# Row sums of 64 MiB: the last fifteen columns scaled on GpSimd, and every load tile on a 1024-byte boundary of SBUF

## The chip, the cores and the metric

The kernel runs on one core of one Trainium2 chip. The metric is device time in microseconds (us) of one execution; the profile's span is some 1.6 us shorter, as it runs from the first to the last instruction. Executions of one kernel on one chip scatter over 0.15 to 0.3 us, now and then more, and the whole change moves a quarter of a microsecond. So the times are read together with the profile, in which the duration of one instruction repeats to some 10 ns, and the stretch from the row's sum to the final sum to some 30 (1.40 to 1.43 us in the seven profiles below whose ends are alike).

## The reference

```python
def setup_inputs():
    batch, seq, dim = 32, 512, 1024
    return {"x": np.random.randn(batch, seq, dim).astype(np.float32), "divisor": float(dim)}

def reference(x, divisor):
    return (np.sum(x, axis=-1) / divisor).astype(np.float32)
```

16,384 rows of 1,024 fp32 are summed and scaled: 128 rows per partition, 67.1 MB in, 64 KB out.

## The kernel before

The first 112 rows of each partition stream through three big rotating buffers in loads of 14 rows. The last 16 come in ever smaller loads (8, 4, 2, 1 rows, then one row in three pieces pa, pb, pc), so that little work is left after the last byte. VectorE (DVE) sums most, ScalarE (ACT) some rows of the end.

```python
main = [(2, 0)] + [(14, 0)] * 6 + [(14, 4), (12, 5)]     # rows of a load, of which on ScalarE
last = [(8, 4), (4, 2), (2, 1)]
bulk = ctx.enter_context(tc.tile_pool(name="bulk", bufs=3))    # t: [P, 14, D], 57,344 B a partition
one = ctx.enter_context(tc.tile_pool(name="one", bufs=1))
res = one.tile([P, M], F32, name="res")
fin = one.tile([P, L], F32, name="fin")
q = one.tile([P, L], F32, name="q")
r = one.tile([P, L], F32, name="r")
nc.gpsimd.memset(r, 0.0)
# ... (t4, t2, row, pa, pb, pc are allocated behind these, at their loads)
c = 768
load(row, x_last[:, j, :])
act_sum(r[:, j : j + 1], row[:, c:], by=scale)                  # ScalarE
nc.vector.reduce_sum(out=q[:, j : j + 1], in_=row[:, :c], axis=AX)
a, b = 448, 704
load(pa, x_last[:, L - 1, :a]); load(pb, x_last[:, L - 1, a:b])  # (cut to two lines)
load(pc[:, : D - b], x_last[:, L - 1, b:])
# ... (res is scaled on GpSimd and stored)
act_sum(pc[:, D - b : D - b + 1], pa)
nc.vector.reduce_sum(out=pc[:, D - b + 1 :], in_=pb, axis=AX)
nc.vector.scalar_tensor_tensor(out=fin[:, : L - 1], in0=q[:, : L - 1], scalar=scale,
                               in1=r[:, : L - 1], op0=MULT, op1=ADD)
nc.vector.tensor_scalar(out=scaled, in0=pc, scalar1=scale, scalar2=0.0, op0=MULT, op1=ADD,
                        accum_out=fin[:, L - 1 :])               # the "final sum"
tc.keep_in_program_order(nc.sync.dma_start(out=o_last, in_=fin))
```

In the built program the three big buffers start 128 bytes past a 256-byte boundary of SBUF. The tiles t4, t2, row, pa, pb and pc, behind 640 bytes of small tiles, happen to start on one.

## Time and profile before

| | before |
|---|---|
| time, three runs | 161.41 us (161.30 to 161.44) |
| span of the profile | 159.8 us |
| row (last but one) landed | 156.16 us |
| pb, pc landed (landing records) | 157.02, 157.50 us |
| final sum started | 157.79 us |

The prediction below shows the lines that carry this. One more pair of DVE's timeline (columns: start, duration, instruction, idle time before it and its releaser):

```profile
106.47 15.09 DVE L153 TENSOR_REDUCE res<-t 128x14 f32<-128x14336 f32 x1 [1.85 <-DMA t<-in_x_dram]
123.41 10.82 DVE L153 TENSOR_REDUCE res<-t 128x10 f32<-128x10240 f32 x1 [1.85 <-DMA t<-in_x_dram]
```

From the first 14-row tile at 21.76 (shown in the prediction) to 123.41 there are six tiles in 101.65 us, 16.942 us each.

### The profile page before, as it was taken

To read this page: it belongs to the slowest core of one execution; us is meant where nothing else is said; L and a number is where in the kernel's file an instruction comes from. 1 tells how busy PE (TensorE), PEld (TensorE's weight loads), DVE (VectorE), ACT (ScalarE), POOL (GpSimd) and SP (SyncE) were. 2 spreads that over 40 slices of the span, in tenths; PEclk is the share of its full clock that TensorE was granted. 3 is DMA by queue.
4 is the path that set the end of the run, shared out by engine and by line. 5 is a ranking of instruction groups with operands and counts; after the bars stand their busy time and mean duration, and the time that the engine had idled before them with its cause. 6 is when DMAs were issued, how large, how long until landed. Compare 5 with 4: busy or idle time off the path is not lost.

```text
span 159.8 us, 139 instructions
## 1 busy us (share of the span) xinstructions
DVE 121.1 (76%) x17; ACT 19.6 (12%) x37; POOL 0.8 (0%) x6
## 2 busy tenths in 40 slices
DVE  0500059995999599978999599959995996494985
ACT  3000000000000000000000000000001900480973
POOL 0000000000000000000000000000000000001000
DMA  7999999978999999978999999978999999899993
GB/s 250 472 459 459 459 459 459 459 330 359 459 459 459 459 459 459 459 316 373 459 459 459 459 459 459 416 345 388 459 459 427 394 480 505 353 435 390 408 400 132
DMA packets 2592, 67.18 MB, mean 420 GB/s; under 512 B 544, under 2 KB 928, under 8 KB 1056
## 3 DMA queue, kind: packets, MB, share of 16 engines
q1 hardware_dynamic: 2592, 67.18, 98.0%
HBM read 67.11 MB, written 0.07 MB: 420 GB/s over the span
## 4 chain that ended last, share of the span: by engine, by line
DMA 76%; DVE 22%; SPq 1%; issue 0%; DVEq 0%
DMA t<-in_x_dram 56%; DMA row<-in_x_dram 21%; DVE res L153 20%; SPq L142 1%; DVE q L176 1%; DVE scaled L198 0%; DVE pc L193 0%; DVE fin L194 0%; DVEq L198 0%; DVEq L232 0%
## 5 line engine op out<-in xcount | busy, mean ns | idle before, releaser
L153 DVE TENSOR_REDUCE res<-t 128x14 f32<-128x14336 f32 (+3 forms) x9 | 111.2, 12360 | 34.3 <-DMA t<-in_x_dram 34.3
L147 ACT ACTIVATE junk<-t 128x1024 f32<-128x1024 f32 x16 | 16.2, 1013 | 135.9 <-DMA t<-in_x_dram 135.9
L153 DVE TENSOR_REDUCE q<-t 128x4 f32<-128x4096 f32 (+2 forms) x3 | 7.9, 2642 | 2.7 <-DMA t<-in_x_dram 2.5
L147 ACT ACTIVATION_READ_ACCUMULATOR junk<-t 128x1 f32 x16 | 3.0, 187 | 0.0
L147 ACT ACT_TABLE_LOAD x1 | 1.3, 1283 | 1.7 <-PEq L218 1.7
L189 POOL TENSOR_SCALAR res<-res 128x112 f32<-128x112 f32 x1 | 0.5, 494 | 143.8 <-DVE res L153 143.8
L176 DVE TENSOR_REDUCE q<-row 128x1 f32<-128x768 f32 x1 | 1.0, 953 | 0.0
L198 DVE TENSOR_SCALAR_CACHE_REDUCE scaled<-pc 128x322 f32<-128x322 f32 x1 | 0.5, 490 | 0.1
L147 ACT ACTIVATE junk<-pa 128x448 f32<-128x448 f32 x1 | 0.5, 548 | 0.0
L193 DVE TENSOR_REDUCE pc<-pb 128x1 f32<-128x256 f32 x1 | 0.4, 414 | 0.0
L147 ACT ACTIVATE junk<-row 128x256 f32<-128x256 f32 x1 | 0.4, 388 | 0.1
L194 DVE SCALAR_TENSOR_TENSOR fin<-q,r 128x15 f32<-128x15 f32 x1 | 0.2, 176 | 0.0
L147 ACT ACTIVATION_READ_ACCUMULATOR junk<-pa 128x1 f32 x1 | 0.2, 186 | 0.0
L147 ACT ACTIVATION_READ_ACCUMULATOR junk<-row 128x1 f32 x1 | 0.2, 185 | 0.0
L139 POOL MEMSET r<- 128x16 f32 x1 | 0.1, 112 | 1.3 <-POOLq L218 1.3
L218 POOL MEMSET const-bfloat16-1.0<- 128x1 bf16 x1 | 0.1, 103 | 0.0
L218 POOL MEMSET const-uint8-127<- 128x1 uint8 x1 | 0.1, 102 | 0.0
L218 POOL MEMSET const-float32-0.0<- 128x1 f32 x1 | 0.1, 99 | 0.2 <-issue 0.2
L218 POOL MEMSET const-float32-1.0<- 128x1 f32 x1 | 0.1, 99 | 0.0
L198 DVE DVE_READ_ACCUMULATOR scaled<-pc 128x1 f32 x1 | 0.1, 83 | 0.0
## 6 DMA issues: line engine op xcount, KB each, us to landing
t<-in_x_dram SPq DMA_DIRECT2D x7, 7168.0 KB, 35.7
t<-in_x_dram SPq DMA_DIRECT2D x1, 6144.0 KB, 33.3
t<-in_x_dram SPq DMA_DIRECT2D x1, 4096.0 KB, 26.1
t<-in_x_dram SPq DMA_DIRECT2D x2, 1024.0 KB, 18.6
t<-in_x_dram SPq DMA_DIRECT2D x1, 2048.0 KB, 30.5
row<-in_x_dram SPq DMA_DIRECT2D x1, 512.0 KB, 33.2
pa<-in_x_dram SPq DMA_DIRECT2D x1, 224.0 KB, 33.3
pc<-in_x_dram SPq DMA_DIRECT2D x1, 160.0 KB, 33.1
```

The lines of the kernel that those rows point to most:

```text
L139: nc.gpsimd.memset(r, 0.0)
L142: tc.keep_in_program_order(nc.sync.dma_start(out=dst, in_=src))
L147: nc.scalar.activation(junk[:, :n], src, COPY, scale=by, accum_out=dst)
L153: nc.vector.reduce_sum(out=dst[:, :d], in_=t[:, :d, :], axis=AX)
L176: nc.vector.reduce_sum(out=q[:, j : j + 1], in_=row[:, :c], axis=AX)
L189: nc.gpsimd.tensor_scalar_mul(out=res, in0=res, scalar1=scale)
L193: nc.vector.reduce_sum(out=pc[:, D - b + 1 :], in_=pb, axis=AX)
L194: nc.vector.scalar_tensor_tensor(out=fin[:, : L - 1], in0=q[:, : L - 1], scalar=scale, in1=r[:, : L - 1], op0=MULT, op1=ADD)
L198: nc.vector.tensor_scalar(out=scaled, in0=pc, scalar1=scale, scalar2=0.0, op0=MULT, op1=ADD, accum_out=fin[:, L - 1 :])
L218: nc = _bacc.Bacc("TRN2", target_bir_lowering=False, num_devices=1)
```

## The change

The intent is twofold. DVE's scaling of fifteen columns stands between the row's sum and the pb sum, at the end where the chain of waits is DVE alone; it goes to GpSimd, and 64 more columns of the row go to ScalarE. And a pad of 896 bytes, with the small tiles moved behind the load tiles, puts each tile that a load writes on a 1024-byte boundary.

```diff
+    pad = ctx.enter_context(tc.tile_pool(name="pad", bufs=1))
+    pad.tile([P, 224], F32, name="pad")
     bulk = ctx.enter_context(tc.tile_pool(name="bulk", bufs=3))
 ...
+    t4 = one.tile([P, 4, D], F32, name="t4")
+    t2 = one.tile([P, 2, D], F32, name="t2")
+    row = one.tile([P, D], F32, name="row")
+    a, b = 448, 704
+    pa = one.tile([P, 512], F32, name="pa")[:, :a]
+    pb = one.tile([P, b - a], F32, name="pb")
+    pc = one.tile([P, D - b + 16], F32, name="pc")[:, : D - b + 2]
     res = one.tile([P, M], F32, name="res")
 ...
-    r = one.tile([P, L], F32, name="r")
-    nc.gpsimd.memset(r, 0.0)
+    r = one.tile([P, 16], F32, name="r")[:, :1]
 ...
-    c = 768
+    c = 704
     load(row, x_last[:, j, :])
-    act_sum(r[:, j : j + 1], row[:, c:], by=scale)
+    act_sum(r, row[:, c:], by=scale)
 ...
-    nc.vector.scalar_tensor_tensor(
-        out=fin[:, : L - 1], in0=q[:, : L - 1], scalar=scale, in1=r[:, : L - 1], op0=MULT, op1=ADD
+    nc.gpsimd.tensor_scalar_mul(out=fin[:, :j], in0=q[:, :j], scalar1=scale)
+    nc.gpsimd.tensor_scalar(
+        out=fin[:, j : j + 1], in0=q[:, j : j + 1], scalar1=scale, scalar2=r, op0=MULT, op1=ADD
     )
```

More of the change, by code (lines that the diff above doesn't have):

```diff
@@ L165 @@
         else:
-            t = one.tile([P, rows, D], F32, name=f"t{rows}")
+            t = t4 if rows == 4 else t2
         load(t, x_last[:, j : j + rows, :])
@@ L169 @@
         j += rows
-    c = 768
-    row = one.tile([P, D], F32, name="row")
+    c = 704
     load(row, x_last[:, j, :])
-    act_sum(r[:, j : j + 1], row[:, c:], by=scale)
+    act_sum(r, row[:, c:], by=scale)
     nc.vector.reduce_sum(out=q[:, j : j + 1], in_=row[:, :c], axis=AX)
-    a, b = 448, 704
-    pa = one.tile([P, a], F32, name="pa")
-    pb = one.tile([P, b - a], F32, name="pb")
-    pc = one.tile([P, D - b + 2], F32, name="pc")
     load(pa, x_last[:, L - 1, :a])
```

## The prediction

> **What bounds the kernel now.** I first read the page's DMA rows and queue row, because a sum over 64 MiB ought to be bound by its loads.
>
> ```profile
> DVE 121.1 (76%) x17; ACT 19.6 (12%) x37; POOL 0.8 (0%) x6
> ...
> DMA  7999999978999999978999999978999999899993
> ...
> q1 hardware_dynamic: 2592, 67.18, 98.0%
> HBM read 67.11 MB, written 0.07 MB: 420 GB/s over the span
> ```
>
> The reader should see that the queue is busy for 98% of 16 engines' span, while VectorE (DVE) is busy for 76% and GpSimd (POOL) for nothing. The sevens in the DMA row look like holes in the stream, so the next view was DVE's timeline, to see whether they are real.
>
> ```profile
> 21.76 15.09 DVE L153 TENSOR_REDUCE res<-t 128x14 f32<-128x14336 f32 x1 [14.65 <-DMA t<-in_x_dram]
> 38.71 15.09 DVE L153 TENSOR_REDUCE res<-t 128x14 f32<-128x14336 f32 x1 [1.87 <-DMA t<-in_x_dram]
> 55.65 15.09 DVE L153 TENSOR_REDUCE res<-t 128x14 f32<-128x14336 f32 x1 [1.84 <-DMA t<-in_x_dram]
> 72.59 15.09 DVE L153 TENSOR_REDUCE res<-t 128x14 f32<-128x14336 f32 x1 [1.86 <-DMA t<-in_x_dram]
> ```
>
> Columns are start, duration, instruction, idle time before it and its releaser. Each reduce starts when its tile lands, 16.94 or 16.95 us after the one before, and the one that spans the first seven (32 to 40 us) comes after the same 16.94 us. The sevens are therefore an effect of binning whole row packets of 2.1 us. A tile is 128 x 57,344 B = 7.34 MB, so the stream runs at 7.34 MB / 16.94 us = 433 GB/s without a gap. DVE idles 1.85 us a tile: nothing that shortens its work in the main loop can help.
>
> So only two things set the end: when the last loads land, and what follows them. The end is in the chain of waits and the timeline.
>
> ```profile
> 122.91 33.25 DMA row<-in_x_dram
> 156.16 0.02 issue
> 156.18 0.96 DVE q L176
> 157.14 0.03 issue
> 157.17 0.18 DVE fin L194
> 157.34 0.34 DVE pc L193
> 157.68 0.04 DVEq L198
> 157.72 0.07 issue
> 157.79 0.49 DVE scaled L198
> ```
>
> ```profile
> 156.18 0.39 ACT L147 ACTIVATE junk<-row 128x256 f32<-128x256 f32 x1
> ...
> 156.72 0.55 ACT L147 ACTIVATE junk<-pa 128x448 f32<-128x448 f32 x1
> 157.17 0.18 DVE L194 SCALAR_TENSOR_TENSOR fin<-q,r 128x15 f32<-128x15 f32 x1
> 157.20 0.19 ACT L147 ACTIVATION_READ_ACCUMULATOR junk<-pa 128x1 f32 x1
> 157.26 0.41 DVE L193 TENSOR_REDUCE pc<-pb 128x1 f32<-128x256 f32 x1
> 157.79 0.49 DVE L198 TENSOR_SCALAR_CACHE_REDUCE scaled<-pc 128x322 f32<-128x322 f32 x1
> ...
> 158.31 0.34 SPq L201 DMA_DIRECT2D out_dram<-fin  x1
> ```
>
> ```profile
> pc<-in_x_dram SPq DMA_DIRECT2D x1, 160.0 KB, 33.1
> pb<-in_x_dram SPq DMA_DIRECT2D x1, 128.0 KB, 33.1
> ```
>
> The penultimate row lands at 156.16. From there the chain is DVE alone: sum of 768 columns, fifteen-column scaling, sum of pb, final scaled sum. The last piece, pc, was issued at 124.39 and landed 33.1 later, at 157.49 (pb: 123.87 + 33.1 = 156.97). The final sum thus starts about 0.30 us after its data is there: this slack is what the change can win from DVE. ScalarE's share is in at 157.20 + 0.19 = 157.39, GpSimd has been idle since 146.
>
> [...] In the built program the three big buffers start at byte 16,512, which is 128 past a boundary, but the tiles t4, t2 and row stand at multiples of 256 (768 past a multiple of 1024). The packet records give a median of 309 ns for the first load's 8,192-byte rows (off boundary) and 309 ns for each of t2's 128 (on one). [...]
>
> **The change part by part.**
>
> *Scaling moves to GpSimd.* DVE loses one instruction. By starts it costs 157.26 - 157.17 = 0.09 us, plus 0.03 of issue before it; without it the pb sum no longer waits for the row's sum to be visible, only for pb at 156.97. GpSimd gains two: fourteen columns, which can run from about 156.2, and one column with a per-partition addend, which needs the row's sum. GpSimd's only comparable instruction, 128x112, took 494 ns. I take 0.3 to 0.5 us for each, an estimate from that row.
>
> *Split of the row, 768 to 704 on DVE.* DVE's slope from its own rows: (1220 - 953) ns / (1024 - 768) = 1.04 ns a column, so 64 columns are 0.067 us. ScalarE's slope: (548 - 388) / (448 - 256) = 0.83 ns, so it gains 0.053 us; its row part with the readout then ends near 156.74, its pa sum near 157.44.
>
> *The new end, landings unchanged.* Row sum 156.18 + 0.886 = 157.07; pb sum starts then or up to 0.05 earlier, as DVE overlapped the start of the last pair by 0.09; it ends about 157.45 to 157.48; the same 0.12 us of semaphore and issue as now, so the final sum starts near 157.58 instead of 157.79. pc at 157.49 and ScalarE at 157.44 are both in. Gain about 0.21 us, capped near 0.27 by pc. GpSimd's last instruction would run from about 157.15 to 157.65, well before the final sum is read out at 158.28 - 0.21 = 158.07: hidden.
>
> *Alignment.* All loads stay in the same order and sizes. The packets fit bytes at 27.2 GB/s per engine plus about 8 ns: 8,192 B is 301 + 8 = 309, and 57,344 B is 2,108 + 8 = 2,116, the most frequent record. Each engine moves 16 loads x 8 rows = 128 such packets, so the whole overhead is 128 x 8 ns = 1.05 us. If half of it[...] came from misalignment, 0.60 us would go; if it is fixed, nothing. The equal 309s argue for nothing, with one reservation: no load tile of before stands on 1024, so a rule that needs 1024 is untested. I count 0.1 us on average.
>
> *Removed memset of r, and the pad.* The memset ran on idle GpSimd at the start, and the pad is never touched: zero. The order of instructions shows the same three loads hoisted ahead of the body and the same queue order after them.
>
> Sum: 161.41 - 0.21 - 0.10 = 161.1 us.
>
> **The rivals.** First, *alignment pays in full*: every landing moves up to 0.6 us forward, the tail follows as a block, the end is near 161.41 - 0.21 - 0.60 = 160.6. For it: the stream sets the end, so any saving in it counts in full. Against it: the equal packet times[...]. Second, *GpSimd becomes the last*: its two instructions, or a slow read of the addend r, end after DVE's final sum. It would need more than 158.07 - 157.15 = 0.9 us for one column, nearly twice its 112-column instruction; each tenth beyond is a tenth lost, so 161.3 to 161.6. Third, *pc's landing or ScalarE takes the place of DVE*: the gain is cut to what the new wait allows. pc caps it at 0.27 and so does not bite; ScalarE would, only if its pa sum slipped past 157.5 (now 157.39, expected 157.44). That would give 161.25 to 161.35. Fourth, the removed work changes nothing because the store waits elsewhere: the earlier result store, queued behind all loads, must also land before the last store; in the event records it does at 157.73, before 158.07, so it does not bite either.
>
> **Range and chances.** The tail alone with no alignment gain, 161.2, gets some 60%; some alignment gain, down to 160.6, about 25%; a new wait or chip-to-chip scatter above 161.35 about 15%. The three runs of before spread over 0.14 us. I say 161.1 us, with 160.5 to 161.4 for eight in ten. Two per cent is 3.2 us, and neither the stream[...] nor a tail of 3.6 us offers that: 2% for faster, 1% for slower, 97% for within 2%.
>
> **What would show it.** In the profile of the changed kernel, the 14-row reduces should still start 16.94 us apart. If alignment pays in full, they should start 8 x 4.7 ns = 0.04 us closer, at 16.90, and the row should land near 155.6. The row's reduce should last 0.886 us, the pb sum follow it without a gap, and the final sum start 0.2 us sooner after the row's landing: 1.42 us instead of 1.63. GpSimd should show two short instructions ending before the final sum. I would be wrong if the last store is released by GpSimd, if ScalarE or pc ends DVE's last wait before a start later than 157.7, or if the spacing of the big tiles changes by more than 0.1 us.

The sum: 161.41 - 0.21 - 0.10 = 161.1 us. Its 0.21 is worked out from the trace of before; its 0.10 is the weighing between nothing and 0.60. The 0.60 is an estimate, and not quite the half it is called: 128 bytes more in a packet, the buffers' displacement, would take 4.7 ns at the 27.2 GB/s that the packets fit, and an engine has 128 packets; that a displaced start costs as much was a supposition. That the stream at 433 GB/s had little left to give, and that GpSimd would not hold DVE up, were assumptions: the trace of before shows neither.

## The result, and the profile after

161.11 us median of six runs (161.04 to 161.20), against 161.32 (161.24 to 161.44) for the kernel before in six runs: ratio 0.9986, 95% interval 0.9973 to 0.9999. Run again beside the displaced kernels below, it gave 161.02 (160.97 to 161.25) against 161.38: ratio 0.9979 (0.9967 to 0.9991). A ratio is the mean time of one kernel's fast runs over that of the other's of the same rounds, so not quite the ratio of the quoted medians. The gain is 0.2 to 0.35 us, within 2%.

The page of the changed kernel: GpSimd has one instruction more on balance, the stream is as full as before.

```profile
DVE 120.9 (76%) x16; ACT 19.6 (12%) x37; POOL 1.2 (1%) x7
...
q1 hardware_dynamic: 2592, 67.18, 98.1%
```

DVE's timeline of the changed kernel, first and seventh 14-row tile:

```profile
21.77 15.09 DVE L163 TENSOR_REDUCE res<-t 128x14 f32<-128x14336 f32 x1 [14.60 <-DMA t<-in_x_dram]
...
123.31 10.82 DVE L163 TENSOR_REDUCE res<-t 128x10 f32<-128x10240 f32 x1 [1.88 <-DMA t<-in_x_dram]
```

101.54 us for the same six tiles, 16.923 each: 0.02 us closer, 0.11 us over the six. The end of the timeline:

```profile
156.12 0.89 DVE L185 TENSOR_REDUCE q<-row 128x1 f32<-128x704 f32 x1
156.17 0.26 POOL L199 TENSOR_SCALAR fin<-q 128x14 f32<-128x14 f32 x1 [10.10 <-DVE q L163]
...
156.98 0.42 DVE L198 TENSOR_REDUCE pc<-pb 128x1 f32<-128x256 f32 x1
157.10 0.27 POOL L200 TENSOR_SCALAR fin<-q,r 128x1 f32<-128x1 f32 x1 [0.67 <-DVE q L185]
157.12 0.19 ACT L157 ACTIVATION_READ_ACCUMULATOR junk<-pa 128x1 f32 x1
157.52 0.49 DVE L204 TENSOR_SCALAR_CACHE_REDUCE scaled<-pc 128x322 f32<-128x322 f32 x1
157.93 0.08 DVE L204 DVE_READ_ACCUMULATOR scaled<-pc 128x1 f32 x1
158.04 0.34 SPq L207 DMA_DIRECT2D out_dram<-fin  x1
```

The row's sum takes 0.886 us instead of 0.953 and the pb sum overlaps its end. From the start of the row's sum to that of the final sum (the tail, below) it is now 157.52 - 156.12 = 1.40 us; before it was 157.79 - 156.18 = 1.61. Both GpSimd instructions lie beside DVE's work and end at 157.37, 0.65 us before the final sum has been read out at 158.01. The last store goes out at 158.04 instead of 158.31: 0.27 us, of which 0.21 is the tail and 0.06 the earlier landing of row.

### The profile page after: what moved, and what is told of

Read it like the earlier page. It is cut to its first block, busy times and chain, and to the rows that moved or that the text cites. A ratio compares the mean times of both kernels' runs of the same rounds, so it can differ in the third digit from the quotient of the medians.

```text
span 159.5 us, 140 instructions
## 1 busy us (share of the span) xinstructions
DVE 120.9 (76%) x16; ACT 19.6 (12%) x37; POOL 1.2 (1%) x7
## 4 chain that ended last, share of the span: by engine, by line
DMA 76%; DVE 22%; SPq 0%; issue 0%; DVEq 0%
DMA t<-in_x_dram 76%; DVE res L163 20%; DVE q L163 1%; DVE q L185 1%; SPq L152 0%; DVE scaled L204 0%; DVE pc L198 0%; DVEq L204 0%; DVEq L238 0%
## 5 line engine op out<-in xcount | busy, mean ns | idle before, releaser
L185 DVE TENSOR_REDUCE q<-row 128x1 f32<-128x704 f32 x1 | 0.9, 886 | 0.0
## 6 DMA issues: line engine op xcount, KB each, us to landing
pc<-in_x_dram SPq DMA_DIRECT2D x1, 160.0 KB, 33.1
```

## The experiments

All twelve kernels gave correct results. Six were to part the gain and test its limits; five displace or place tiles; one is the changed kernel again. "Row sum" and "final sum" are starts in DVE's timeline of the one profile of each kernel, and the difference is that of the rounded starts. The runs were three jobs on three chips, each with the kernel before in it; only the job with the changed kernel again (and 512, 128 and 32 past) had the changed kernel too, so the other differences from it go across chips.

| kernel | time, us (range) | ratio to before (95%) | row sum | final sum | difference |
|---|---|---|---|---|---|
| before | 161.32 to 161.38 by job | 1 | 156.18 | 157.79 | 1.61 |
| changed | 161.11 (161.04 to 161.20) | 0.9986 (0.9973 to 0.9999) | 156.12 | 157.52 | 1.40 |
| changed, again | 161.02 (160.97 to 161.25) | 0.9979 (0.9967 to 0.9991) | 156.01 | 157.44 | 1.43 |
| layout alone | 161.18 (161.09 to 161.29) | 0.9989 (0.9976 to 1.0002) | 156.08 | 157.69 | 1.61 |
| arithmetic alone | 161.10 (161.04 to 161.24) | 0.9985 (0.9973 to 0.9997) | 156.16 | 157.56 | 1.40 |
| layout and split | 161.30 (161.07 to 161.80) | 1.0000 (0.9988 to 1.0012) | 156.01 | 157.55 | 1.54 |
| split at 640 | 161.01 (160.96 to 161.47) | 0.9984 (0.9972 to 0.9996) | 156.05 | 157.48 | 1.43 |
| 512 past 1024 | 160.97 (160.94 to 161.24) | 0.9977 (0.9964 to 0.9990) | 156.02 | 157.45 | 1.43 |
| 128 past | 161.39 (161.31 to 161.56) | 1.0001 (0.9989 to 1.0013) | 156.34 | 157.85 | 1.51 |
| 32 past | 161.52 (161.47 to 162.15) | 1.0015 (1.0003 to 1.0027) | 156.60 | 158.14 | 1.54 |
| 224 past | 161.47 (161.41 to 161.55) | 1.0008 (0.9996 to 1.0020) | 156.46 | 157.98 | 1.52 |
| pad alone | 161.32 (161.16 to 161.89) | 1.0005 (0.9992 to 1.0019) | 156.03 | 157.64 | 1.61 |
| GpSimd once more | 161.09 (160.99 to 161.34) | 0.9985 (0.9972 to 0.9998) | 156.29 | 157.70 | 1.41 |
| GpSimd four times more | 161.95 (161.84 to 162.03) | 1.0038 (1.0026 to 1.0049) | 156.14 | 157.55 | 1.41 |

My theory after the result was that the tail gives 0.20 us and the layout some 0.07. The rivals: the layout is the whole gain, or the tail is and the earlier landings are scatter.

### Layout alone

The changed kernel with the old arithmetic (in its text, against the changed kernel):

```diff
-    c = 704
+    c = 768
-    nc.gpsimd.tensor_scalar_mul(...); nc.gpsimd.tensor_scalar(...)
+    nc.vector.scalar_tensor_tensor(...)          # with r [P, 16] zeroed, as before
```

> The layout of the changed kernel (all load tiles on 1024-byte boundaries), the arithmetic of the kernel before: DVE does the fifteen-column scaling, the row is split at 768. My theory (the tail gives 0.20 us, the alignment some 0.07): about 0.05 to 0.10 us faster than before, the final sum starting 1.6 us after the row's landing as before, and 57,344-byte packet records of 2116 ns in over 90% of cases instead of 63%. Rival one (the alignment is the whole gain, the tail is capped elsewhere): 0.2 us faster. Rival two (the earlier landings in the profile of the changed kernel are scatter from run to run): 0.00 and packet records spread as before.

The end of its timeline:

```profile
156.08 0.95 DVE L186 TENSOR_REDUCE q<-row 128x1 f32<-128x768 f32 x1
...
157.69 0.49 DVE L204 TENSOR_SCALAR_CACHE_REDUCE scaled<-pc 128x322 f32<-128x322 f32 x1
```

The tail is the old one, 1.61 us, and everything comes 0.10 us sooner. 161.18 against 161.34 is somewhat more than I expected, but the interval reaches 1.0002, so the times alone don't settle it. That the layout acts is shown by the packet records (a packet is one row of a load: the trace has 7 x 128 of 57,344 bytes): 93% (830 of 896) of the 57,344-byte rows took 2116 ns, as expected, against 63% before. The spacing of the big tiles, worked out as above, says the same in all fourteen profiles: 16.91 to 16.93 us in the nine with the big buffers on a multiple of 256 bytes, 16.94 in the three at 128 past, 16.95 in the two at 32 and 224.

### Arithmetic alone

The kernel before with the GpSimd scaling and c = 704, its tiles where they were.

> The layout of the kernel before (big buffers 128 bytes past a boundary), the arithmetic of the changed kernel: GpSimd scales, the row is split at 704. My theory: about 0.20 us faster than before, the final sum starting 1.42 us after the row's landing, packet records spread as before (63% at 2116 ns). Rival one (alignment is the whole gain): no faster than before.

```profile
156.16 0.89 DVE L175 TENSOR_REDUCE q<-row 128x1 f32<-128x704 f32 x1
...
157.56 0.49 DVE L198 TENSOR_SCALAR_CACHE_REDUCE scaled<-pc 128x322 f32<-128x322 f32 x1
```

Row lands as late as before, the tail is 1.40 us as in the changed kernel, the time is 161.10 against 161.34. The rival by which the layout is the whole gain falls. As 161.10 is also the time of the changed kernel (161.11 and 161.02), the times show no clear gain of the layout beside the new arithmetic. 66% of the packets took 2116 ns, spread as before.

### Layout and split, scaling still on DVE

```diff
-    nc.gpsimd.tensor_scalar_mul(...); nc.gpsimd.tensor_scalar(...)
+    nc.vector.scalar_tensor_tensor(...)          # c stays 704
```

> The changed kernel with the fifteen-column scaling put back on DVE; the split stays at 704, the layout aligned. It parts the tail's gain in two. My theory: the split is worth 0.067 us of DVE time and nothing caps it, the move to GpSimd 0.13: so 0.13 us slower than the changed kernel, final sum 1.56 us after the row's landing. Rival (the landing of pb already holds the pb sum in the changed kernel, so the split alone is what moved): within 0.05 us of the changed kernel.

The tail is 1.54 us, so it parts as expected: 0.07 for the 64 columns, and 0.11 to 0.14 for the instruction taken off DVE (by which profile of the changed kernel one compares). The time is inconclusive: its profiled execution took 161.07, the others 161.27 to 161.80, so this kernel's median is burdened by scatter that its tail doesn't explain.

### Split at 640

```diff
-    c = 704
+    c = 640
```

> The changed kernel with the row split at 640: 64 columns more from DVE to ScalarE. My theory: in the changed kernel the pb sum starts 0.02 us after pb has landed, so a shorter row sum on DVE only adds idle time: no gain, within 0.03 us of the changed kernel, and DVE shows an idle gap of some 0.05 us before the pb sum with DMA pb as releaser. ScalarE's pa sum still ends before the pb sum. Rival (DVE is still the bound of the tail): another 0.067 us faster.

```profile
156.05 0.82 DVE L185 TENSOR_REDUCE q<-row 128x1 f32<-128x640 f32 x1
...
156.95 0.42 DVE L198 TENSOR_REDUCE pc<-pb 128x1 f32<-128x256 f32 x1
```

The row's sum ends at 156.87 and the pb sum starts at 156.95: a gap of 0.07 us, though the timeline names no releaser for one that short. The landing records have pb complete at 156.92. In the changed kernel they have it at 156.955, and its pb sum starts at 156.979, before the row's sum ends at 157.002; in all ten profiles with the scaling on GpSimd the pb sum starts 23 or 24 ns after pb's landing record. The tail is 1.43 us, no shorter than with 704, and 161.01 is the changed kernel's 161.02 to 161.11. So in the changed kernel the bound of the tail has already passed from DVE to the landing of pb; more work taken off DVE there is worth nothing.

### The changed kernel again, and 512, 128, 32 and 224 bytes past

Only the pad's length is changed, so all load tiles move together:

```diff
-    pad.tile([P, 224], F32, name="pad")      # 224 fp32: every load tile on a 1024-byte boundary
+    pad.tile([P,  96], F32, name="pad")      # 512 bytes past one (still on a multiple of 256)
+    pad.tile([P, 256], F32, name="pad")      # 128 bytes past
+    pad.tile([P, 232], F32, name="pad")      # 32 bytes past
+    pad.tile([P, 280], F32, name="pad")      # 224 bytes past
```

> The changed kernel once more, beside the three displaced ones on the same chip. Row lands near 156.06 (155.98 to 156.10 in the profiles of aligned kernels so far), over 87% of the 57,344-byte packet records at 2116 ns, time 161.0 to 161.2.

> The changed kernel with a shorter pad: every load tile starts 512 bytes past a 1024-byte boundary, still on a multiple of 256. Theory one (256 bytes is what counts): packet records and row landing as in the aligned kernel, 2116 ns in about 90%. Theory two (1024 is what counts): records spread as in the kernel before, 65% at 2116, row landing 0.06 us later.

> The changed kernel with a longer pad: every load tile starts 128 bytes past a 1024-byte boundary, as the big buffers of the kernel before do. Both theories: packet records spread (65% at 2116 ns for 57,344-byte rows, some 20% at 1213 for 32,768-byte rows), row landing 0.06 us later than aligned. If the tiles t4, t2, row and the pieces were only on 256 before and are now off it, theory one adds little, since those are 15 of 128 packets' worth of time. A rival (the order of tiles in memory, not the boundary, gave the earlier landings): as aligned.

> The changed kernel with every load tile 32 bytes past a 1024-byte boundary. If what counts is whether a row starts on the boundary at all, as off_128. If what counts is the number of bytes past it[...], different from off_128 by up to a few ns a packet[...], which the landings would show.

> The changed kernel with every load tile 224 bytes past a 256-byte boundary, the mirror of the 32-byte case. Reading one[...]: the mean of the 8,192-byte records goes from 309 (aligned) over 312.9 (128 past) further up, and the time is over 161.6. Reading two[...]: as 128 or better than 32 past, 161.3 to 161.5.

From the last two the author's reasons why a displaced start might cost are cut. What they leave to be tested is whether the cost changes with the number of bytes past the boundary (for 224 past, reading one: the more bytes, the slower) or not (reading two).

512 past (160.97 us) is as good as the boundary (161.02), so 1024 is not what counts. 128 past costs 161.39 - 161.02 = 0.37 us, the whole gain. In its timeline row comes 0.33 us later, where I had expected 0.06, and the pb sum waits for its late piece too, which lengthens the tail by 0.08:

```profile
156.34 0.89 DVE L185 TENSOR_REDUCE q<-row 128x1 f32<-128x704 f32 x1
...
157.31 0.42 DVE L198 TENSOR_REDUCE pc<-pb 128x1 f32<-128x256 f32 x1
```

32 and 224 past cost 0.50 and 0.45 us, and they look alike in the packets (none and one quick row of 128 in the 12-row load, none and none in the 8-row load), so the number of bytes past the boundary is not what is paid for. The next table counts, among the 128 rows of each load, those that took the smallest usual time (2116 ns for a 14-row load, then 1815, 1213, 611 and 309 ns for 12, 8, 4 and 2 rows). It is worked out from the trace's packet records.

| kernel | 14-row loads, first to seventh | 12 rows | 8 rows | t4 | t2 |
|---|---|---|---|---|---|
| before (big buffers 128 past, t4 and t2 on 256) | 124, 115, 102, 96, 56, 34, 36 | 46 | 44 | 121 | 128 |
| layout alone (all on 1024) | 128, 124, 116, 116, 110, 112, 124 | 99 | 128 | 128 | 128 |
| 512 past | 123, 117, 108, 105, 108, 93, 112 | 95 | 128 | 128 | 128 |
| 128 past | 127, 113, 92, 91, 69, 40, 38 | 51 | 46 | 44 | 43 |
| 32 past | 127, 114, 84, 14, 3, 0, 0 | 0 | 0 | 0 | 13 |
| 224 past | 128, 121, 83, 13, 6, 0, 0 | 1 | 0 | 0 | 15 |
| pad alone (big on 1024, t4 and t2 128 past 256) | 127, 119, 111, 101, 113, 106, 117 | 96 | 128 | 128 | 128 |

Nearly nothing is lost in the first 14-row load at any of the addresses tried (123 to 128 quick rows of 128); off the 256-byte multiple the slow rows come with time and then stay. A slow row mostly takes 2 to 11 ns more. The mean over the 8-row load is 1213.0 ns on a boundary, 1216.0 at 128 past and 1218.1 at 32 or 224.

### The pad alone

```diff
+    pad = ctx.enter_context(tc.tile_pool(name="pad", bufs=1))
+    pad.tile([P, 224], F32, name="pad")
     bulk = ctx.enter_context(tc.tile_pool(name="bulk", bufs=3))
```

This puts the big buffers of the kernel before on the boundary and, as nothing else moves, pushes the small load tiles off theirs.

> The kernel before with the 896-byte pad alone: the big buffers now on 1024-byte boundaries, but the small tiles stay ahead of the rest, so t4, t2, row and the pieces, which stood on multiples of 256 before, now stand 128 bytes past one. My theory (what counts is 256 bytes, for every load): 57,344-byte records tight (over 87% at 2116 ns), the small tiles' records spread, the stream between row and pc slower; the gain on the big tiles (0.07 us at the row's landing) is lost in the last pieces: 0.0 to 0.2 us slower than before, and 0.1 us or more slower than the aligned kernel with the same arithmetic (161.18). Rival (only the big buffers count): as that kernel, 0.1 us faster than before.

The packets went otherwise than I expected. Those of the small tiles are as tight as on a boundary (last line of the table), and row comes as early as in the best kernels (row sum at 156.03). With the 128-past kernel, whose t4 and t2 are slow, and with the kernel before, whose t4 and t2 recover as soon as they stand on 256, the finding for the packets becomes: in these kernels most rows of a load were slow only when it started off the 256-byte multiple and a long stream of such rows had gone before it (quick rows in t4 and t2: 44 and 43 of 128 at 128 past, 128 and 128 with the pad alone, 121 and 128 before).

The landings went as I expected. pb's landing record is 0.99 us behind row's, as with all tiles displaced (0.97 to 1.00), against 0.86 to 0.89 in the ten other profiles. In this kernel that is hidden, since pb lands at 157.00 and DVE, busy with the scaling, starts its sum at 157.11. What grows is the lag from a load's last packet to its landing record, in ns:

| kernel | 12 rows | t4 | row | pa | pb |
|---|---|---|---|---|---|
| before | 460 | 436 | 327 | 298 | 274 |
| changed, again | 337 | 308 | 327 | 300 | 298 |
| 128 past | 457 | 462 | 479 | 509 | 521 |
| pad alone | 343 | 346 | 425 | 485 | 503 |

Within a few small loads it grew off the 256-byte multiple (pad alone: 346 to 503 ns from t4 to pb) and shrank on it (before: 436 to 274). At 128 past it is 0.22 of the 0.41 us by which pb lands later than in the changed kernel; later packets are the rest. So small tiles off the multiple cost something too where the end waits for their landing, as at 128 past, whose tail is 0.08 us longer.

The time settles less: three executions took 161.16 to 161.20, as the layout alone does, and three 161.44 to 161.89. I can't say what the slower three met, nor whether it is the layout at all; there is one profile, of a quick one.

### GpSimd's last instruction repeated

```diff
+    nc.gpsimd.tensor_scalar(                   # once more, or four times more, with the same operands
+        out=fin[:, j : j + 1], in0=q[:, j : j + 1], scalar1=scale, scalar2=r, op0=MULT, op1=ADD
+    )
```

> The changed kernel with GpSimd's last instruction (one column, 0.27 us) done twice. My theory: GpSimd's last result is in at 157.37, 0.65 us before DVE's final sum at 158.02, so a second one (0.27 us and a semaphore hop of under 0.1) stays hidden: the same time as the changed kernel, 160.95 to 161.15, the last store still released by DVE. Rival (GpSimd is already the last or close to it): 0.3 us slower.

> The changed kernel with GpSimd's last instruction done five times, each waiting for the one before. My theory: four more at 0.27 to 0.37 us each put GpSimd's end 1.1 to 1.5 us later, past the slack of 0.65: 0.45 to 0.85 us slower than the changed kernel, and the drain before the last store is released by GpSimd. Rival (the last store waits for DVE alone): no change in time, and the result may be wrong.

Once more is hidden: 161.09 against the changed kernel's 161.02 to 161.11. Its end of the timeline:

```profile
157.64 0.27 POOL L203 TENSOR_SCALAR fin<-q,r 128x1 f32<-128x1 f32 x1
157.70 0.49 DVE L207 TENSOR_SCALAR_CACHE_REDUCE scaled<-pc 128x322 f32<-128x322 f32 x1
158.12 0.08 DVE L207 DVE_READ_ACCUMULATOR scaled<-pc 128x1 f32 x1
```

Four times more puts GpSimd last. Its timeline, and then the line of SyncE's own waits that is new:

```profile
157.96 0.08 DVE L216 DVE_READ_ACCUMULATOR scaled<-pc 128x1 f32 x1
158.22 0.26 POOL L209 TENSOR_SCALAR fin<-q,r 128x1 f32<-128x1 f32 x1
158.58 0.27 POOL L212 TENSOR_SCALAR fin<-q,r 128x1 f32<-128x1 f32 x1
158.93 0.34 SPq L219 DMA_DIRECT2D out_dram<-fin  x1
```

```profile
SPq L250 <- POOL fin L212: 1.2, 1, 1.2
```

The chained instructions start 0.36 us apart (0.27 and 0.09 of issue), four of them are 1.44 us, and less the slack of 0.65 this leaves 0.79. Measured against the changed kernel's 161.02 to 161.11 it is 0.84 to 0.93, at the upper end of my 0.45 to 0.85 and just over it (against the run with one more, of the same job, it is 0.86). The store goes out 0.09 us after GpSimd's end, where it had gone out 0.03 after DVE's, which adds 0.06 to the 0.79. That the last store waits for DVE alone is refuted: it goes out after GpSimd. So the slack is real and of about the stated size. The final sum lasted 0.49 us with GpSimd running beside it, as without.

No kernel here beats the changed one beyond scatter: 512 past (160.97) and the split at 640 (161.01) equal it.

## Why the prediction was right

The forecast of 161.1 us within 160.5 to 161.4 held: 161.11 and 161.02. By its steps:

- *The stream has no holes and sets the landings.* Right. Tiles come every 16.92 us after as every 16.94 before, although the DMA row of the page still shows sixes and sevens.
- *Scaling off DVE and the split, 0.21 us.* Right: the tail went from 1.61 to 1.40 us. The sum of the row took 0.886 us, ScalarE's part 0.441 (0.388 + 0.053), both as computed. The two parts are about 0.07 and 0.14 in this order, by the kernel that keeps the scaling on DVE; the scaling moved alone, with the split at 768, wasn't run, and what the split adds to it is not shown. ScalarE's pa sum did not slip by the 0.053: it starts 23 ns after pa's landing record before and after, so it waits for pa and not for ScalarE's part of the row.
- *GpSimd hidden.* Right, with more to spare than said: 0.26 and 0.27 us instead of 0.3 to 0.5, ending 0.65 us before DVE. The runs with one and with four more show the slack's size. The rival "GpSimd becomes the last" would need two more such instructions, an estimate from the slack of 0.65 us and the 0.36 a repeat. GpSimd did not hold DVE up by more than 6 ns: the pb sum took 420 ns with GpSimd beside it and 414 in the kernel before; the final sum took 0.49 us with GpSimd beside it, in the runs with one and with four more, and 490 ns in the kernel before. GpSimd's 14 columns took 262 ns and its 112 took 495: on one line, an estimate from these two, 2.4 ns a column (DVE's sum of the row: 1.04) above a fixed 0.23 us.
- *What caps the tail next.* Wrong. The prediction named pc's landing, at 0.27 us. It is the landing of pb, which came into force at once: with the row split at 640 the tail gets no shorter. The prediction put pb at 156.97, from an issue time and a rounded 33.1; the landing record says 157.02. With it and the 24 ns that follow a landing, the pb sum could not start before 157.04, and the prediction's row sum ends at 157.07 less an overlap of up to 0.05. The two bounds lie within 0.03 us of each other, so that the size of 0.21 came true although another wait set it is partly luck.
- *Alignment, 0.1 us on average.* The size is of the right order, but not pinned down: six tiles take 0.08 to 0.17 us less by the spacing; row lands 0.04 to 0.17 us sooner than in the kernel before in eight profiles of kernels with the big buffers on 256, and 0.11 later in the ninth (GpSimd once more); the layout alone gained 0.16 in time with an interval reaching zero, and beside the new arithmetic no gain is shown. The argument was not right. "The equal 309s argue for nothing" compared the first load's rows, off the boundary, with t2's, on it. The table shows why this could not tell: the first 14-row load was quick at every address tried (123 to 128 rows of 128), and most rows were slow only later in a stream off the 256-byte multiple (34 and 36 quick ones in the last two 14-row loads of before). The reservation, "a rule that needs 1024 is untested", fell as well: 512 past is as good (160.97 against 161.02). The layout gives so little partly because the small tiles already stood on multiples of 256 before: the new arithmetic with the tiles of before took 161.10, with every tile 128 past 161.39.
- *The rival of full payment, 0.60 us through 4.7 ns saved in each packet.* It falls: in the first 14-row load the rows took 2116 ns both on and off the boundary (128 of 128 and 124), and the spacing of tiles shrank by 0.02 us, not 0.04. (128 x 8 ns is 1.02 us, not the 1.05 of the prediction; 128 x 4.7 ns is 0.60.)

What makes rows slow in a long stream off the boundary stays open. The records show the state build up (from 124 to 36 quick rows of 128 before, to none at 32 past) and go at once when a load stands on 256 (121 quick rows in t4 before, after 44 in the 8-row load), while the lag of the landing fades over several loads (from 436 ns at t4 to 274 at pb). They don't show what causes it.

## What to carry to other kernels

At the end of a load-bound kernel, time the steps after the last landings one by one and move to an idle engine what the last store needs but the last sum doesn't; then look which landing is the next bound before moving more. Put tiles that a long stream writes, and the small ones of its end, on multiples of 256 bytes: it costs a pad, and here up to half a microsecond in 161 hung on it (161.52 us with every load tile 32 bytes past, 161.02 on the boundary). Don't judge an alignment by the first loads of a trace, as its cost can build up later (at 32 past from 127 quick rows of 128 in the first 14-row load to none in the sixth); and when a change gives a few tenths of a microsecond, judge it by steps in the profile that repeat to 10 or 30 ns, beside times that scatter by 200.
